# A decoder trunk's FFN down projection as a one-level Strassen product

## The chip, the cores and the metric

The kernel runs on one core of a Trainium2 chip. The metric is the device time of one execution in microseconds (us). Five engines work side by side, each with its own instruction stream: TensorE (PE, with its weight loads shown apart as PEld), VectorE (DVE), ScalarE (ACT), GpSimd (POOL) and SyncE (SP), which issues the DMAs.

## The reference

A trunk of two layers works on 512 tokens of width 1024 in float32. Layer 0 mixes tokens with a gated linear recurrence (HGRN2), layer 1 with sliding-window attention. Each mixer is followed by the same kind of feed-forward network, with D_FF = 2816, and a residual add:

```python
def conv_ffn(x, w_up, conv_w, conv_b, w_down):
    gate, val = jnp.split(x @ w_up, 2, axis=-1)
    gp = jnp.pad(gate, ((0, 0), (CONV_WIDTH - 1, 0), (0, 0)))
    conv = conv_b
    for j in range(CONV_WIDTH):
        conv = conv + conv_w[j] * gp[:, j:j + s_]
    return (jax.nn.silu(conv) * val) @ w_down
...
    h = h + conv_ffn(rms_norm(h, ffn_norm[layer]), ...)
```

The change is in the last product, `(...) @ w_down`: 512 tokens x 2816 features times 2816 x 1024 weights, in each layer. After layer 0 the residual stream goes into two norms (the shared K/V and the attention); after layer 1 into the final norm.

## The kernel before

All activations stand feature-major, as tiles of 128 features x 512 tokens. `h` holds the residual stream as eight such tiles. A product in near-float32 accuracy is made of three matmuls in the fp32r format: each operand x is split into a rounded part xh (an ACT copy) and the rest xl = x - xh (a DVE subtraction), and `three` (lines 103 to 106) adds hi*xh, hi*xl and lo*xh in PSUM. Weights come in raw by a DMA on SP's queue into one of four `raw` buffers of 128 x 1024, and `weights` (lines 91 to 101) makes `whi` (L99, ACT) and `wlo` (L100, DVE) from them, three buffers each. `project` loops over the k-tiles of one output tile.

The FFN has 22 tiles of 128 features. `hidden` makes one: 24 matmuls for the gate, 24 for the value, each with 512 columns, then the convolution on DVE (L497 to L502), SiLU on ACT (L503), a scaling on POOL (L504), the product with the value from PSUM on DVE (L505) and the split of the result (L507, L508). `up` makes a chunk of tiles, `down` multiplies the chunk with its rows of the weights: for each of the eight output tiles one PSUM bank, three matmuls a feature tile, and then `residual`: one DVE add of the bank to `h` (L192) and, where a norm follows, `norm.feed`: for each gain of the norm a scaled rounding on ACT (L138) and a split on DVE (L139), and a square on ACT (L147) that POOL adds up (L151). Layer 0 runs in two chunks of 11 tiles, and the second feeds the norm with two gains. Layer 1 runs in chunks of 10 and 8; its last four tiles go through `down_out`, which works on halves of 256 tokens and ends the kernel.

PSUM has eight banks: two under the tag `mm`, two under `bk`, which `any_bank` hands out in turn, and two pairs under `ax`. SBUF has 40 slots of 128 x 512 (`slot`) for the split activations. The order of instructions on an engine is set when the program is built, by a scheduler that may put an instruction ahead of earlier ones that are not ready; on the chip each engine works through its own list in that order.

Of the kernel before, what the change touches and what calls it, by code (L numbers as in the profile page):

```python
# [15 lines left out]
P = 128  # L16
# [28 lines left out]

@with_exitstack
def trunk(ctx: ExitStack, tc: tile.TileContext, xT, vec, w_qf, w_ig, w_ho, w_kv, w_q, w_o,
          w_up, w_dn, con, msk, out):
    nc = tc.nc
    V, A, G, PE = nc.vector, nc.scalar, nc.gpsimd, nc.tensor  # L50

# [15 lines left out]
    def slot(dt=F32):  # L67
        return act.tile([P, S], dt, tag="a", name=nm("a"))
# [12 lines left out]
    def any_bank():  # L81
        turn[0] += 1
        return mm_bank() if turn[0] % 2 else bk_bank()
# [107 lines left out]
    def residual(ps, m, norm):  # L191
        V.tensor_tensor(h[:, m], h[:, m], ps, op=ALU.add)  # L192
        if norm is not None:
            norm.feed(m)

    def project(ps, src, xs, n=KT, first=True, last=True, after={}):
        hi, lo = weights(src, n * P)
        for k in range(n):
            ks = slice(k * P, (k + 1) * P)
            three(ps, hi[:, ks], lo[:, ks], *xs[k], first and k == 0, last and k == n - 1)  # L200
            if k in after:
                after[k]()

# [1 line left out]
    norm = Norm([V_HG])  # L205

    lbe = small.tile([P, 2, HEADS], F32, tag="lbe", name="lbe", bufs=1)
# [276 lines left out]
        pair = aux_pair().rearrange("p (i a) b -> p i (a b)", i=2)  # L484
        return [pair[:, 0], pair[:, 1]]

# [1 line left out]
    def hidden(l, j, norm):  # L488
        xs = norm.xs[0]
        pg, pv = any_bank(), any_bank()  # L490
        project(pg, w_up[l, 2 * j], xs)
        if j == 0:
            norm.stats()
        project(pv, w_up[l, 2 * j + 1], xs, after={3: norm.spread} if j == 0 else {})
        gp = work("ks", (P, S + 2), 4)
        G.memset(gp[:, 0:2], 0.0)  # L496
        V.tensor_tensor(gp[:, 2:S + 2], pg, norm.bc, op=ALU.mult)  # L497
        cw = [col(V_CW + (l * 3 + i) * FT + j) for i in range(3)]
        c = work("qp", (P, S), 4)
        V.tensor_scalar(c, gp[:, 0:S], cw[0], col(V_CB + l * FT + j), op0=ALU.mult, op1=ALU.add)  # L500
        for i in (1, 2):
            V.scalar_tensor_tensor(c, gp[:, i:S + i], cw[i], c, op0=ALU.mult, op1=ALU.add)  # L502
        A.activation(c, c, AF.Silu)  # L503
        G.tensor_tensor(c, c, norm.bc, op=ALU.mult)  # L504
        V.tensor_tensor(c, pv, c, op=ALU.mult)  # L505
        uh, ul = slot(F32R), slot(F32R)
        A.copy(uh, c)  # L507
        V.tensor_tensor(ul, c, uh.bitcast(F32), op=ALU.subtract)  # L508
        return uh, ul

    def up(l, norm, j0, j1):
        return [hidden(l, j, norm) for j in range(j0, j1)]

    def down(l, hid, j0, nxt=None):
        n = len(hid)
        cut = n if n * P <= 1024 else (n + 1) // 2
        for m in range(KT):
            ps = any_bank()
            for a, b in ((0, cut), (cut, n)):
                if a < b:  # L520
                    project(ps, w_dn[l, m, :, (j0 + a) * P:(j0 + b) * P], hid[a:b], b - a,
                            a == 0, b == n)
            residual(ps, m, nxt)

    def down_out(l, hid, j0):
        n = len(hid) * P
        ws = []
        for m in range(KT):
            raw = wraw.tile([P, 1024], F32, tag="raw", name=nm("raw"))
            nc.sync.dma_start(raw[:, 0:n], w_dn[l, m, :, j0 * P:j0 * P + n])  # L530
            hi, lo = slot(F32R), slot(F32R)
            A.copy(hi[:, 0:n], raw[:, 0:n])
            V.tensor_tensor(lo[:, 0:n], raw[:, 0:n], hi[:, 0:n].bitcast(F32), op=ALU.subtract)
            ws.append((hi, lo))
# [70 lines left out]
    for m in (6, 7):  # L605
        Out(w_ho, m, m, [any_bank()]).run(mixed, nf)
    na = Norm([V_KV, V_AT])
    down(0, up(0, nf, 0, 11), 0)
    down(0, up(0, nf, 11, FT), 11, na)

# [1 line left out]
    halves = [slice(0, HD), slice(HD, P)]  # L612
    heads = lambda ap, g: ap.rearrange("p (t d) -> p t d", t=NT)[:, :, g * HD:(g + 1) * HD]
    k_hi, k_lo, v_hi, v_lo = ([slot(F32R) for _ in range(2)] for _ in range(4))
# [185 lines left out]
        o4.step(k, mixed[k])  # L800
    o4.close(nf)
    Out(w_o, 7, 7, [mm_bank()]).run(mixed, nf)
    down(1, up(1, nf, 0, 10), 0)
    hid = [up(1, nf, 10, 18), up(1, nf, 18, FT)]
    down(1, hid[0], 10)
    down_out(1, hid[1], 18)


def _pieces(w):
    """[K, N] -> per 128 columns: [N/128, 128 rows in the k-tile, K/128, 128]."""  # L810
    k, n = w.shape
    return np.ascontiguousarray(
        w.reshape(k // P, P, n // P, P).transpose(2, 1, 0, 3).reshape(n // P, P, k))


def _out_pieces(w):
    t = w.reshape(KT, P, D)
    a = t[:, :, :512].reshape(4, 2, P, 512).transpose(0, 2, 1, 3).reshape(4, P, D)
    b = t[:, :, 512:768].reshape(2, 4, P, 256).transpose(0, 2, 1, 3).reshape(2, P, D)
    return np.concatenate([a, b, _pieces(w)[6:]])  # L820


def _constants():
# [13 lines left out]
def _layout(x, hg_norm, hg_w_in, hg_lb_logits, hg_out_norm, hg_w_out, kv_norm, w_kv, attn_norm,  # L837
# [12 lines left out]
                           for j in range(8)])  # L850
    up = [np.stack([_pieces(w[:, :FF]), _pieces(w[:, FF:])], axis=1).reshape(2 * FT, P, D)
          for w in ffn_w_up]
    dn = [_pieces(w) for w in ffn_w_down]
    con, msk = _constants()
    arrays = dict(
        xT=x[0].T.reshape(KT, P, S).transpose(1, 0, 2), vec=vec, w_qf=qf, w_ig=ig,
        w_ho=_out_pieces(hg_w_out[0]), w_kv=_pieces(w_kv), w_q=_pieces(attn_w_q[0][:, perm]),
        w_o=_out_pieces(attn_w_o[0][perm]), w_up=np.stack(up), w_dn=np.stack(dn), con=con, msk=msk)
    return {k: np.ascontiguousarray(v) for k, v in arrays.items()}


# [14 lines left out]
```

## Time and profile before

| what | value |
|---|---|
| time, median of 3 runs (lowest to highest) | 1226.41 us (1226.07 to 1227.5) |
| profiled execution, span from first to last instruction | 1224.9 us |
| what lies around the span (median less span) | 1.5 us |
| PE busy | 1205.3 us (98%) |
| DVE, ACT, POOL busy | 58%, 37%, 14% |
| read from HBM | 102.33 MB, 85 GB/s over the span |

The span is the time from the first instruction's start to the last one's end in the one execution that was profiled. A share of busy time is an average over the whole span. Matmuls are pipelined and their ends are modelled, so the price of a matmul is read from the distance of one start to the next and not from its duration.

### The profile page before, as it was taken

The numbers are of one execution on the slowest core, as the hardware profiler recorded it, in microseconds if no ns is written. First come the engines' busy times: TensorE is split into PE (matmuls) and PEld (weight loads), VectorE is DVE, ScalarE is ACT, GpSimd is POOL, SyncE is SP. The second block draws the span as 40 slices with busy tenths as digits, with TensorE's granted clock in tenths as the row PEclk, the third lists the DMA queues.
The fourth block names the chain that finished last, engine by engine and source line by source line (L and its number), as shares of the span: only waits on it lengthen the run. The fifth ranks groups of instructions, "written<-read, shape, count | busy, mean of one in ns | idle before, by whom it ended". The sixth has DMA issues, their size and how long they took to land.

```text
span 1224.9 us, 15849 instructions
## 1 busy us (share of the span) xinstructions
PE 1205.3 (98%) x6154; PEld 1005.1 (82%) x6154; DVE 714.4 (58%) x1257; ACT 447.4 (37%) x814; POOL 176.2 (14%) x238
## 2 busy tenths in 40 slices
PE   8999999999999999999999999999999999999997
PEld 6888888888888888888888888887888888888886
DVE  7767676667555543555554778737555435565434
ACT  5433333325323222223233576734322222232223
POOL 3000000013201100001101243403101000111001
PEclk9999999999999999999999999999999999999998
DMA  7222222213233224333233311113322343323212
GB/s 241 73 69 70 70 70 70 69 35 104 87 95 94 77 82 116 103 92 99 76 84 115 104 36 53 35 52 104 103 86 71 87 119 103 103 86 103 83 55 69
DMA packets 34939, 105.45 MB, mean 86 GB/s; under 512 B 3760, under 2 KB 7088, under 8 KB 34864
## 3 DMA queue, kind: packets, MB, share of 16 engines
q1 hardware_dynamic: 33776, 103.40, 27.8%
q8 instruction: 48, 0.79, 0.3%
q10 hardware_dynamic: 1088, 1.05, 0.3%
q14 instruction: 27, 0.22, 0.1%
HBM read 102.33 MB, written 2.10 MB: 85 GB/s over the span
## 4 chain that ended last, share of the span: by engine, by line
PE 90%; DVE 4%; ACT 3%; issue 1%; POOL 1%; DMA 0%; SPq 0%; DVEq 0%; ACTq 0%; POOLq 0%
PE mm L104 13%; PE mm L106 13%; PE mm L105 13%; PE bk L104 11%; PE bk L106 11%; PE bk L105 11%; PE mm L251 7%; PE ax L319 3%; PE ax L106 2%; PE ax L104 2%; PE ax L105 2%; ACT ks L693 1%; DVE wlo L100 1%; ACT qp L693 1%; PE ax L378 1%
## 5 line engine op out<-in xcount | busy, mean ns | idle before, releaser
L99 ACT CAST whi<-raw 128x1024 fp32r<-128x1024 f32 (+3 forms) x208 | 199.1, 959 | 411.4 <-PE mm L105 184.1
L104 PE MATMUL mm<-a,whi 128*128 128x512 f32 x720 | 288.0, 400 | 0.0
L106 PE MATMUL mm<-a,wlo 128*128 128x512 f32 x720 | 285.8, 397 | 0.0
L105 PE MATMUL mm<-a,whi 128*128 128x512 f32 x720 | 285.2, 396 | 0.0
L100 DVE TENSOR_TENSOR wlo<-raw,whi 128x1024 fp32r<-128x1024 f32 (+3 forms) x208 | 237.6, 1143 | 68.8 <-ACT whi L99 68.7
L104 PE MATMUL bk<-a,whi 128*128 128x512 f32 x560 | 222.0, 396 | 0.0
L105 PE MATMUL bk<-a,whi 128*128 128x512 f32 x560 | 221.1, 395 | 0.3 <-DVE a L139 0.3
L106 PE MATMUL bk<-a,wlo 128*128 128x512 f32 x560 | 221.2, 395 | 0.0
L106 PEld LDWEIGHTS mm<-a,wlo 128*128 128x128 f32 x720 | 135.9, 189 | 31.1
L104 PEld LDWEIGHTS mm<-a,whi 128*128 128x128 f32 x720 | 136.0, 189 | 29.0 <-issue 0.2
L105 PEld LDWEIGHTS mm<-a,whi 128*128 128x128 f32 x720 | 136.0, 189 | 29.0 <-issue 0.2
L105 PEld LDWEIGHTS bk<-a,whi 128*128 128x128 f32 x560 | 105.5, 188 | 25.6 <-DVE a L139 0.7
L104 PEld LDWEIGHTS bk<-a,whi 128*128 128x128 f32 x560 | 105.5, 188 | 24.7 <-issue 0.5
L106 PEld LDWEIGHTS bk<-a,wlo 128*128 128x128 f32 x560 | 105.5, 188 | 24.5
L251 PE MATMUL mm<-whi,a 128*128 128x256 f32 x512 | 93.7, 283 | 0.0
L251 PEld LDWEIGHTS mm<-whi,a 128*128 128x128 f32 x512 | 79.5, 189 | 1.0 <-PE mm L123 0.4
L251 PE MATMUL mm<-wlo,a 128*128 128x256 f32 x256 | 72.5, 283 | 3.4 <-DVE wlo L100 3.4
L503 ACT ACTIVATE qp<-qp 128x512 f32<-128x512 f32 x44 | 27.8, 632 | 127.9 <-DVE qp L502 127.9
L504 POOL TENSOR_TENSOR qp<-qp,rbc 128x512 f32<-128x512 f32 x44 | 56.8, 1292 | 100.8 <-ACT qp L503 100.8
L496 POOL MEMSET ks<- 128x2 f32 x44 | 4.3, 100 | 448.7 <-DVE qp L502 435.2
L502 DVE SCALAR_TENSOR_TENSOR qp<-ks,vecs,qp 128x512 f32<-128x512 f32 x88 | 65.9, 749 | 1.7
L251 PEld LDWEIGHTS mm<-wlo,a 128*128 128x128 f32 x256 | 48.2, 188 | 4.6 <-DVE wlo L100 4.3
(198 smaller groups left out, 1395.6 us busy)
## 6 DMA issues: line engine op xcount, KB each, us to landing
raw<-in_w_up_dram SPq DMA_DIRECT2D x88, 512.0 KB, 3.5
raw<-in_w_dn_dram SPq DMA_DIRECT2D x32, 320.0 KB, 2.9
raw<-in_w_qf_dram SPq DMA_DIRECT2D x16, 512.0 KB, 3.6
raw<-in_w_ig_dram SPq DMA_DIRECT2D x14, 512.0 KB, 3.6
raw<-in_w_dn_dram SPq DMA_DIRECT2D x16, 384.0 KB, 3.2
raw<-in_w_ho_dram SPq DMA_DIRECT2D x8, 512.0 KB, 3.5
raw<-in_w_q_dram SPq DMA_DIRECT2D x8, 512.0 KB, 3.4
raw<-in_w_o_dram SPq DMA_DIRECT2D x8, 512.0 KB, 3.6
```

What stands on the lines that cost most here:

```text
L99: A.copy(hi[:, c], raw[:, c])
L100: V.tensor_tensor(lo[:, c], raw[:, c], hi[:, c].bitcast(F32), op=ALU.subtract)
L104: PE.matmul(ps, ah, bh, start=first, stop=False)
L105: PE.matmul(ps, ah, bl, start=False, stop=False)
L106: PE.matmul(ps, al, bh, start=False, stop=last)
L251: PE.matmul(ps, x[:, ts], w[:, ws], start=k == 0 and t % 2 == 0 and i == 0, stop=k == KT - 1 and t % 2 == 1 and i == 2, skip_group_check=True)
L319: PE.matmul(ps[:, c, 0:width], ks[:, c * P:(c + 1) * P], mv[:, c, 0:width], start=True, stop=True)
L378: PE.matmul(ps[r, c * b:(c + 1) * b], ks[:, o:o + b], qp[:, o + b:o + 2 * b], start=True, stop=True)
L502: V.scalar_tensor_tensor(c, gp[:, i:S + i], cw[i], c, op0=ALU.mult, op1=ALU.add)
L503: A.activation(c, c, AF.Silu)
L504: G.tensor_tensor(c, c, norm.bc, op=ALU.mult)
L693: A.activation(x, x, AF.Exp, bias=mx[:, n:n + 1], accum_out=den[:, n:n + 1])
```

## The change

The down projection of a pair of FFN tiles onto a pair of output tiles is a product of 2 x 2 blocks, with the 512 tokens cut into a left and a right half of 256. Instead of eight block products of 256 tokens the new kernel makes seven, each of three matmuls, from sums of weight blocks and of activation blocks (the form with S1 to S4 on the weights and four sums on the activations). `up_pairs` replaces `up` and makes the activation sums: half on DVE (`s3`), the others on POOL (`t13`, `t24`), and splits three tiles and a half in place of two. `blocks` loads four weight blocks (256 KB), makes four sums in three POOL adds, and splits 896 columns. `down` goes over four pairs of outputs; a pair uses four PSUM banks (mm and bk, or the two ax pairs, in turn), and its results are put together by eight DVE operations and one ACT copy. Chunks are of six tiles, and the last one of layer 0 of four; the last four tiles of layer 1 go through `down_out` as before, with their weights from an array of their own. `_quads` lays out the blocks on the host.

```diff
     def hidden(l, j, norm):
...
-        uh, ul = slot(F32R), slot(F32R)
-        A.copy(uh, c)
-        V.tensor_tensor(ul, c, uh.bitcast(F32), op=ALU.subtract)
-        return uh, ul
+        return c
+
+    def parts(x):
+        xh, xl = slot(F32R), slot(F32R)
+        A.copy(xh, x)
+        V.tensor_tensor(xl, x, xh.bitcast(F32), op=ALU.subtract)
+        return xh, xl
...
+    def up_pairs(l, norm, j0, j1):
+        out = []
+        for j in range(j0, j1, 2):
+            a = hidden(l, j, norm)
+            s3 = slot(F32R)
+            A.copy(s3[:, lft], a[:, lft])
+            V.tensor_tensor(s3[:, rgt], a[:, lft], s3[:, lft].bitcast(F32), op=ALU.subtract)
+            t13 = work("st")
+            G.tensor_tensor(t13[:, lft], a[:, lft], a[:, rgt], op=ALU.subtract)
+            b = hidden(l, j + 1, norm)
+            t24 = work("fr")
+            G.tensor_tensor(t13[:, rgt], a[:, rgt], b[:, rgt], op=ALU.subtract)
+            G.tensor_tensor(t24[:, lft], t13[:, rgt], a[:, lft], op=ALU.subtract)
+            G.tensor_tensor(t24[:, rgt], t24[:, lft], b[:, lft], op=ALU.add)
+            (b21, b22), (t1, t3), (t2, t4) = (both(parts(x)) for x in (b, t13, t24))
+            out.append(dict(p1=(s3[:, lft], s3[:, rgt]), p2=b21, p3=b22, p4=t4, p5=t1, p6=t2,
+                            p7=t3))
+        return out
+    A21, A12, A11, A22, S3, S1, S2, S4 = (slice(i * P, (i + 1) * P) for i in range(8))
+    LEFT = (("p1", A11), ("p2", A12), ("p4", A22), ("p3", S4), ("p5", S1), ("p6", S2), ("p7", S3))
+
+    def blocks(src):
...
+        nc.sync.dma_start(raw[:, 0:512], src)
+        two = lambda a, b: raw[:, a:b].rearrange("p (i c) -> p i c", i=2)
+        G.tensor_tensor(two(512, 768), two(256, 512),
+                        raw[:, A21].unsqueeze(1).broadcast_to([P, 2, P]), op=ALU.add)
+        G.tensor_tensor(raw[:, S2], raw[:, S1], raw[:, A11], op=ALU.add)
+        G.tensor_tensor(raw[:, S4], raw[:, S2], raw[:, A12], op=ALU.add)
+        A.copy(hi[:, P:], raw[:, P:])
+        V.tensor_tensor(lo[:, P:], raw[:, P:], hi[:, P:].bitcast(F32), op=ALU.subtract)
+        return hi, lo
 
     def down(l, hid, j0, nxt=None):
-        n = len(hid)
-        cut = n if n * P <= 1024 else (n + 1) // 2
-        for m in range(KT):
-            ps = any_bank()
-            for a, b in ((0, cut), (cut, n)):
-                if a < b:
-                    project(ps, w_dn[l, m, :, (j0 + a) * P:(j0 + b) * P], hid[a:b], b - a,
-                            a == 0, b == n)
-            residual(ps, m, nxt)
+        for q in range(KT // 2):
+            if q % 2 == 0:
+                banks = [mm_bank(), mm_bank(), bk_bank(), bk_bank()]
+            else:
+                banks = aux_two() + aux_two()
+            place = dict(p1=(0, lft), p3=(0, rgt), p2=(1, lft), p5=(1, rgt), p6=(2, lft),
+                         p7=(2, rgt), p4=(3, lft))
+            ps = {k: banks[b][:, s] for k, (b, s) in place.items()}
...
+            for i, x in enumerate(hid):
+                hi, lo = blocks(w_dn[l, j0 // 2 + i, q])
+                for k, w in LEFT:
...
+                    PE.matmul(ps[k], hi[:, w], xh, start=fresh, stop=False, skip_group_check=True)
+                    PE.matmul(ps[k], hi[:, w], xl, start=False, stop=False, skip_group_check=True)
+                    PE.matmul(ps[k], lo[:, w], xh, start=False, stop=last, skip_group_check=True)
+            h0, h1 = h[:, 2 * q], h[:, 2 * q + 1]
+            u = work("state")
+            V.tensor_tensor(h0, h0, banks[0], op=ALU.add)
+            V.tensor_tensor(h0, h0, banks[1], op=ALU.add)
+            V.tensor_tensor(h1[:, lft], h1[:, lft], ps["p4"], op=ALU.add)
+            V.tensor_tensor(h1[:, rgt], h1[:, rgt], ps["p5"], op=ALU.subtract)
+            A.copy(u[:, lft], ps["p6"])
+            V.tensor_tensor(u[:, lft], u[:, lft], ps["p1"], op=ALU.add)
+            V.tensor_tensor(u[:, rgt], u[:, lft], ps["p7"], op=ALU.subtract)
+            V.tensor_tensor(h0[:, rgt], h0[:, rgt], u[:, lft], op=ALU.add)
+            two = lambda x: x.rearrange("p (i t) -> p i t", i=2)
+            V.tensor_tensor(two(h1), two(h1), u[:, rgt].unsqueeze(1).broadcast_to([P, 2, H]),
+                            op=ALU.subtract)
+            for m in (2 * q, 2 * q + 1):
+                if nxt is not None:
+                    nxt.feed(m)
...
-    down(0, up(0, nf, 0, 11), 0)
-    down(0, up(0, nf, 11, FT), 11, na)
+    for j0, j1 in ((0, 6), (6, 12), (12, 18)):
+        down(0, up_pairs(0, nf, j0, j1), j0)
+    down(0, up_pairs(0, nf, 18, FT), 18, na)
...
-    down(1, up(1, nf, 0, 10), 0)
-    hid = [up(1, nf, 10, 18), up(1, nf, 18, FT)]
-    down(1, hid[0], 10)
+    for j0, j1 in ((0, 6), (6, 12)):
+        down(1, up_pairs(1, nf, j0, j1), j0)
+    hid = [up_pairs(1, nf, 12, 18), up(1, nf, 18, FT)]
+    down(1, hid[0], 12)
     down_out(1, hid[1], 18)
```

## Rows read from the trace of the kernel before

**Rows 1.** The page: busy us and share by engine; granted PE clock in 40 slices.

```profile
PE 1205.3 (98%) x6154; PEld 1005.1 (82%) x6154; DVE 714.4 (58%) x1257; ACT 447.4 (37%) x814; POOL 176.2 (14%) x238
...
PEclk9999999999999999999999999999999999999998
```

**Rows 2.** The page: the chain that ended last, by engine.

```profile
PE 90%; DVE 4%; ACT 3%; issue 1%; POOL 1%; DMA 0%; SPq 0%; DVEq 0%; ACTq 0%; POOLq 0%
```

**Rows 3.** Windows: layer 0's first down, its second down, and its first up projection.

```profile
core 0: us, PE busy (x) PEld busy (x) DVE busy (x) ACT busy (x) POOL busy (x), PEclk, DMA share, GB/s
436.40:497.00 60.60, 60.60 (x262) 49.13 (x262) 20.02 (x25) 13.10 (x17) 0.00 (x0) 1.00 0.38 105
620.30:681.00 60.70, 60.70 (x263) 49.23 (x262) 32.84 (x39) 26.09 (x38) 8.52 (x6) 1.00 0.36 104
...
326.00:436.00 110.00, 110.00 (x475) 89.16 (x475) 61.01 (x81) 33.25 (x41) 15.22 (x21) 1.00 0.29 87
```

**Rows 4.** Timeline of DVE in layer 0's first down (start, us, operation).

```profile
450.58 0.69 DVE L192 TENSOR_TENSOR h<-h,bk 128x512 f32<-128x512 f32 x1 [2.13 <-PE bk L106]
451.22 0.96 DVE L100 TENSOR_TENSOR wlo<-raw,whi 128x768 fp32r<-128x768 f32 x1
...
473.60 0.69 DVE L192 TENSOR_TENSOR h<-h,mm 128x512 f32<-128x512 f32 x1 [2.14 <-PE mm L106]
```

**Rows 5.** Timeline of PE in `down_out`, first and last of 36 starts.

```profile
1191.28 0.28 PE L104 MATMUL mm<-a,a 128*128 128x256 f32 x1
...
1195.60 0.28 PE L104 MATMUL bk<-a,a 128*128 128x256 f32 x1
```

**Rows 6.** Groups of instructions by line and shape, whole span: count, busy us, mean ns.

```profile
L504 POOL TENSOR_TENSOR qp<-qp,rbc 128x512 f32<-128x512 f32 x44 | 56.8, 1292 | 100.8 <-ACT qp L503 100.8
...
L508 DVE TENSOR_TENSOR a<-qp,a 128x512 fp32r<-128x512 f32 x44 | 30.2, 686 | 1.4 <-ACT a L507 1.4
...
L138 ACT ACTIVATE a<-h,vecs 128x512 fp32r<-128x512 f32 x40 | 28.4, 716 | 11.4 <-DVE h L192 9.3 <-DMA h<-in_xT_dram 1.6
...
L507 ACT CAST a<-qp 128x512 fp32r<-128x512 f32 x44 | 27.4, 622 | 15.2 <-DVE qp L505 14.9
...
L333 DVE TENSOR_TENSOR qp<-qp,tot 128x256 f32<-128x256 f32 x48 | 20.3, 423 | 4.6 <-PE ax L378 1.8 <-ACT mvb L356 0.5
...
L99 ACT CAST whi<-raw 128x768 fp32r<-128x768 f32 x16 | 13.4, 837 | 37.4 <-PE bk L105 20.8 <-PE mm L105 16.6
...
L545 DVE TENSOR_TENSOR h<-h,bk 128x256 f32<-128x256 f32 x8 | 3.4, 419 | 1.9 <-PE bk L106 1.8
```

**Rows 7.** Timeline of POOL, then of DVE, around four POOL adds.

```profile
835.32 6.72 POOL L151 TENSOR_TENSOR acc<-acc,kst 128x512 f32<-128x512 f32 x4 [6.61 <-ACT kst L147]
...
835.67 0.68 DVE L192 TENSOR_TENSOR h<-h,bk 128x512 f32<-128x512 f32 x1
...
840.88 2.25 DVE L100 TENSOR_TENSOR wlo<-raw,whi 128x1024 fp32r<-128x1024 f32 x1
...
843.64 1.21 DVE L100 TENSOR_TENSOR wlo<-raw,whi 128x1024 fp32r<-128x1024 f32 x1
```

**Rows 8.** Timelines at an FFN tile's end: PE's next matmul, then DVE's product.

```profile
507.55 0.40 PE L104 MATMUL mm<-a,whi 128*128 128x512 f32 x1
...
508.10 0.69 DVE L505 TENSOR_TENSOR qp<-bk,qp 128x512 f32<-128x512 f32 x1 [2.07 <-POOL qp L504]
```

**Rows 9.** Timelines at layer 0's end: DVE feeding the norm, then PE after the K projection.

```profile
651.53 0.75 DVE L139 SCALAR_TENSOR_TENSOR a<-h,vecs,a 128x512 fp32r<-128x512 f32 x1
...
680.64 0.69 DVE L192 TENSOR_TENSOR h<-h,bk 128x512 f32<-128x512 f32 x1
...
686.02 0.28 PE L175 MATMUL ax<-cons,acc 128*128 128x1 f32 x2
```

**Rows 10.** The page: DMA issues, KB each, us from issue to landing.

```profile
raw<-in_w_dn_dram SPq DMA_DIRECT2D x8, 256.0 KB, 2.7
```

## The prediction before the run

> **What bounds the kernel now.** I read the page first: PE is busy for 98% of the span at full granted clock [rows 1], and nine tenths of the chain that ended last is PE [rows 2]. The reader is to see that only PE time counts, as long as the other engines keep PE fed. Then I read the two kinds of stretch that the change touches. In a down projection PE never idles, DVE is a third to a half busy, and POOL does nothing unless a norm is being fed; in an up projection DVE is a little over half busy [rows 3]. Inside a down projection DVE works in short bursts: one residual add, then the low part of a weight tile, and from one residual add to the third after it, 3 x 33 = 99 matmuls, pass 23.02 us, so a 512-column matmul costs 0.2325 us [rows 4]. At the kernel's end the same three-matmul pattern runs with 256 columns: 36 matmuls in 4.32 us, 0.120 us each [rows 5].
>
> **What the change takes from PE.** Before, the projections through `down` hold 22 x 8 x 3 = 528 matmuls in layer 0 and 18 x 8 x 3 = 432 in layer 1: 960 x 0.2325 = 223.2 us. After, a pair of tiles and a pair of outputs is a block of 7 x 3 = 21 matmuls of 256 columns; 11 x 4 and 9 x 4 blocks make 80 x 21 = 1680 matmuls: 1680 x 0.120 = 201.6 us. PE saves 21.6 us. The weight is loaded once for each matmul [rows 1], in both kernels and in the rows, so the price already holds the load. The Trainium skill (TensorE: Matmul & The Clock Gate, Back-to-back issue gap) gives columns / 2.4 plus 2.5 ns: 215.8 and 109.2 ns, and so a saving of 23.7 us. Both rows are some 8 to 10% above that, and I keep the rows' 21.6.
>
> **What it adds to the other engines, per block.** PE needs 21 x 0.120 = 2.52 us. ACT rounds 896 columns, about 0.94 us by the 768-column row; DVE takes the low part of 896 columns, between 0.96 (768) and 1.22 (1024), so 1.09 us; POOL makes the four sums with one add of 256 and two of 128 [rows 6, 7]. No POOL add of these widths is in the trace: scaled from 1.29 us for 512 columns it is 0.65 + 2 x 0.32 = 1.29 us; if a quarter of the 512 price were fixed, 1.94 us. I take 1.5 us, nearer the scaled one. The load is 256 KB in 2.52 us, 104 GB/s, which the down stretches draw already [rows 3], and lands in 2.7 us [rows 10] with four raw buffers ahead: hidden.
>
> **Per quarter (one pair of outputs).** The residual chain is two 512-column adds from PSUM (0.69 each), four 256-column ones from PSUM (0.42), one of 256 (0.42) and one of 512 columns (0.69) with both inputs in SBUF [rows 4, 6]: 4.17 us, against two adds (1.4 us) before. A quarter of a six-tile chunk has three blocks: PE 7.56 us, DVE 3 x 1.09 + 4.17 = 7.44 us. DVE goes from idling half the time to 98%. What sits behind the chain on DVE is the low part of the next weights: `whi`/`wlo` have three buffers, so block i+3 starts on ACT when block i ends on PE, DVE may start about 1.3 us later, and PE needs the result 5.3 us after that end. If the chain runs first it ends some 3.6 us after the block's end and the low part at 4.7: in time by 0.6 us, with nothing else in the way.
>
> **POOL is in the way.** While POOL ran four adds from 835.32 to 842.04, a DVE add that read PSUM kept its 0.68 us, but a weight split with two SBUF inputs took 2.25 us, against 1.21 us for the next, just after POOL stopped; and the POOL adds took 1.68 us each against 1.29 alone [rows 6, 7]. So POOL's adds and DVE's two-SBUF-input operations take turns. In a six-tile chunk (PE 30.2 us) DVE has: the last gate product 0.69, three splits of the last pair 2.06, ten weight splits 10.9, three chains 12.5, two splits for the next up projection 2.4: 28.6 us, of which 9.9 read PSUM. POOL has three adds of the last pair, 2.0, and the sums of the six to eight blocks that four raw buffers don't let it do ahead, 9 to 12 us. Work that must take turns is 18.7 + 11 to 14 = 29.7 to 32.7 us. Below, the loss is 0 (all of it fits); above, if none of POOL's time fell beside a PSUM read, DVE would need 28.6 + 14 = 42.6 us and a chunk would lose 12. Since PSUM reads can cover 9.9 of POOL's 11 to 14, I take a value near full occupancy, 2 us a chunk, 12 us for the six; both ends go to the range, the upper one as 5 a chunk, since 12 would need POOL to work only beside two-input operations.
>
> **Each start of a chunk.** The first quarter takes all four mm/bk banks, and the fourth is the value bank of the last up tile, free when DVE's product ends: started 0.55 us after PE went on, 0.69 us long, so 1.3 us with the hand-over [rows 8]. PE reaches that bank after six matmuls, 0.72 us. Seven starts x 0.6 = 4.2 us (0.4 to 0.8 each). Behind the product stands the chain of the last pair: three POOL adds, a rounding and a split, ready some 5 us after PE went on. Two blocks of cover (5.0 us) hide it in a six-tile chunk; with its one block of cover the four-tile chunk doesn't, which is in its sum below.
>
> **The last chunk of layer 0.** It has two blocks a quarter, PE 8 x 2.52 = 20.2 us, and its residuals feed two gains of the next norm. Before, this feeding lay over 61 us of matmuls [rows 3], 7.67 us an output [rows 4]; it comes in full now. The K projection needs the first gain of all eight tiles, and the second gain of seven stands ahead of it on DVE. From the last up matmul DVE must do: product 0.69, three splits 2.06, six weight splits 6.5, four chains 16.7, one split of the K weights 1.22, fifteen feeds of 0.75 [rows 9] 11.2: 38.4 us. With 0.4 us ahead of it and the last three K matmuls behind (0.7 us) that ends at 39.5 us; PE alone would end at 20.2 + 5.6 = 25.8 us, and before there was no idle time in these 5.6 us (the last residual at 680.64, the K projection done by 686.02) [rows 9]. So at least 13.7 us are lost. POOL's seven square sums (9 us), pair adds and block sums come on top, partly beside 12.9 us of PSUM reads: 0 to 10 us, of which I take 3, near the lower end by the same cover as above. 17 us. ACT has 16 roundings of 0.72 [rows 6] and its other work, some 26 us, below DVE.
>
> **The rest.** `down_out` is unchanged but for its source. Its eight splits of weights (0.69 each) used to lie in DVE's idle time; now the chunk ahead has none, and its first half takes PE 96 x 0.120 = 11.5 us against DVE's last chain 4.2, splits 5.5 and own adds 5.5: 0 to 3.7 us, I take 2. In the up projections a pair adds 1.1 us on DVE, 1.0 on ACT and 2.6 on POOL to 22.3 us of matmuls, beside a DVE that is 55% busy there [rows 3]: nothing; without that cover it would be 1.1 us x 20 pairs. Slots: 16 + 21 + 8 exceed 40 at layer 1's end, so the last tiles' splits wait until the norm's slots come free during tile 21; their consumer is a whole chunk away: nothing.
>
> **Sum.** -21.6 + 12 + 4.2 + 17 + 2 = +13.6 us. The profiled execution spans 1224.9 us; the runs' median is 1226.41, so 1.5 us lie around the span, and I keep them: 1240 us. What a measurement can tell from no change is about 0.2%, 2.5 us.
>
> **Rivals.**
> (a) *DVE and POOL fit, PE alone sets the chunks.* The six-tile chunks and `down_out` lose nothing (the upper figures, 28.6 of 30.2 us, allow it), and the last chunk loses its 13.7, or 8.5 if the second gain's feeds are put off: -21.6 + 4.2 + 13.7 = -3.7, or -8.9 us: 1217 to 1223. For it: 0.6 us of slack in each quarter and sums made early. Against it: the turns of POOL and DVE [rows 7]. It decides if all the six-tile chunks together lose less than about 1 us (6 with the feeds put off). 0.22.
> (b) *Turns in every quarter.* Two-SBUF-input work and POOL strictly one after the other: 3.27 + 1.11 + 3 x 1.5 = 8.9 us against 7.56, in 24 quarters +32 us: -21.6 + 4.2 + 32 + 17 + 2 = +33.6, 1260 us. For it, the 2.25 us split; against it, that the sums of the first four to six blocks and the last chain lie outside the chunk. 0.18. Beside it stands the Trainium skill (SBUF — State Buffer, Who interferes with whom): a VectorE instruction with two SBUF inputs and a GpSimd one that reads SBUF exclude each other for the whole instruction. The trace agrees: 1.04 us were lost in 1.16 us beside POOL.
> (c) *It cancels:* stalls of 19 to 24 us, 1226 us. 0.12.
> That 256-column matmuls cost more than half of the wide ones, so that nothing is saved, [rows 5] exclude.
> My forecast, a few us lost in each chunk and DVE the bound in the last one of layer 0, has 0.48 (its own range 1229 to 1252).
>
> **Numbers.** Faster 0.22 (a), same 0.12 (c), slower 0.48 + 0.18 = 0.66. The range reaches from (a) to (b): 1219 to 1260; some 0.1 lies below and as much above. PE gaps in the last chunk may lower the granted clock, 1.00 in all stretches of [rows 3]; that is part of the upper end.
>
> **What would show it.** Right: 256-column starts 0.120 us apart inside blocks; PE waiting for `wlo` after the second and third quarters of six-tile chunks; weight splits over 2 us beside POOL adds; DVE without idle time from layer 0's last up tile until some 40 us later, and the K projection ending 13 us or more late. Wrong: `wlo` never late, narrow POOL adds well under 1.3 us a block, or an instruction order that puts splits ahead of chains and feeds.

## The result and the profile after

The changed kernel takes 1236.33 us in the median of four executions (1232.21 to 1239.02) against 1226.24 for the kernel before: ratio 1.008, 95% interval 1.0059 to 1.010. It is slower, by 10 us or 0.8%; 1240 us was forecast. The execution that the profile shows is the quickest of the four, 1232.21 us with a span of 1230.4, so its trace explains 5.5 of the 10 us.

The page of the changed kernel, with busy shares, the granted clock in 40 slices and the chain that ended last:

```profile
PE 1192.5 (97%) x6874; PEld 1027.1 (83%) x6874; DVE 891.2 (72%) x1513; ACT 502.3 (41%) x906; POOL 470.8 (38%) x558
...
PEclk9999999999999999999999899999999999999998
...
PE 70%; DVE 12%; POOL 8%; ACT 5%; issue 3%; DMA 2%; SPq 0%; DVEq 0%; POOLq 0%; ACTq 0%
```

Against [rows 1, 2], DVE has risen from 58 to 72% of the span and POOL from 14 to 38%. PE's share of the chain has fallen by 20 points, and 15 of them went to DVE and POOL. The windows of the first down chunk and of the stretch from the last up matmul of layer 0 to the norm's statistics say where:

```profile
core 0: us, PE busy (x) PEld busy (x) DVE busy (x) ACT busy (x) POOL busy (x), PEclk, DMA share, GB/s
379.00:410.80 31.80, 30.80 (x254) 30.14 (x253) 28.82 (x40) 13.90 (x18) 22.37 (x25) 1.00 0.38 115
653.60:701.40 47.80, 36.99 (x215) 32.41 (x213) 43.07 (x60) 25.99 (x40) 19.93 (x20) 0.89 0.27 88
```

Where [rows 3] had PE without a gap and DVE a third to a half busy, a six-tile chunk now has DVE at 28.8 of 31.8 us; in the last chunk of layer 0 DVE works 43.1 of 47.8 us and PE only 37.0, partly at the lower clock. From first start to the chunk's end the six six-tile chunks take 31.8, 32.2, 31.8, 31.7, 31.7 and 31.0 us, against 30.24 of matmuls: 8.8 us lost. The last chunk and the K projection need 20.2 + 5.6 = 25.7 us of matmuls, and their stretch takes 22.1 us more than that. A part comes back in the attention, from one statistics start to the next. The lines are the two starts, then the window of this stretch in the kernel before, in the changed kernel and in the run e2 (below):

```profile
701.35 0.27 PE L175 MATMUL ax<-cons,acc 128*128 128x1 f32 x1 [0.82 <-POOL acc L151]
...
858.31 0.38 PE L175 MATMUL ax<-cons,acc 128*128 128x1 f32 x2 [0.40 <-POOL acc L151]
...
686.02:846.71 160.69, 156.97 (x879) 131.62 (x878) 113.64 (x287) 96.55 (x243) 52.20 (x89) 0.99 0.19 58
701.35:858.31 156.96, 152.14 (x858) 126.42 (x858) 113.58 (x289) 96.51 (x243) 55.04 (x92) 1.00 0.18 58
...
683.87:843.18 159.31, 155.58 (x880) 130.62 (x878) 113.61 (x287) 96.49 (x243) 52.27 (x89) 1.00 0.20 57
```

That is 157.0 us, against 160.7 before (686.02 to 846.71). Two things lie in these 3.7 us. The changed kernel has run 21 matmuls of the V projection, 4.9 us of PE time, ahead of the statistics: its window of the last chunk counts 215 matmuls, where 168 of the product and 24 of the K projection make 192, and its attention counts 21 fewer than before. And the kernel before had a granted clock of 0.99 in its attention against 1.00; e2, with the work of the kernel before there and a clock of 1.00, takes 159.3 us, so about 1.4 of the 3.7 us are not owed to the change, and some 2.3 of the V projection's 4.9 come back. The account -21.6 + 8.8 + 22.1 - 3.7 = +5.6 us meets the spans, 1230.4 - 1224.9 = +5.5.

What PE waits for at the start of a six-tile chunk shows in the timelines of PE, POOL and DVE at the second chunk of layer 1:

```profile
1019.89 0.39 PE L106 MATMUL mm<-a,wlo 128*128 128x512 f32 x1
1020.12 0.28 PE L579 MATMUL mm<-a,whi 128*128 128x256 f32 x1
...
1020.95 0.28 PE L580 MATMUL mm<-a,whi 128*128 128x256 f32 x1
1022.18 0.39 PE L579 MATMUL mm<-a,whi 128*128 128x256 f32 x1 [0.95 <-DVE qp L505]
...
1019.41 0.74 POOL L553 TENSOR_TENSOR raw<-raw 128x256 f32<-128x256 f32 x1
1020.11 1.29 POOL L504 TENSOR_TENSOR qp<-qp,rbc 128x512 f32<-128x512 f32 x1
...
1021.43 0.69 DVE L505 TENSOR_TENSOR qp<-mm,qp 128x512 f32<-128x512 f32 x1 [2.17 <-POOL qp L504]
```

Inside a block the starts are 0.12 us apart, as [rows 5] had it. Then PE stands for 1.1 us until the last tile's product (L505) frees a bank. That product began 0.55 us after PE went on in [rows 8]; here 1.31 us after, because POOL's scaling L504 came behind a block sum (L553). The first two chunks of layer 1 then wait 0.5 us for an operand. In layer 0 a chunk's start shows three shorter waits: 0.3 us for the bank and two for the operands made from `t24`, 1.6 us together. These two are, in the first chunk, the waits for the operand's high part and for its low part:

```profile
385.87 0.39 PE L579 MATMUL bk<-a,whi 128*128 128x256 f32 x1 [0.52 <-ACT a L510]
386.59 0.39 PE L580 MATMUL bk<-a,whi 128*128 128x256 f32 x1 [0.34 <-DVE a L511]
```

The chunk began at 379.08, so the low part was there only some 7.5 us after PE went on. Within the quarters PE waits hardly at all, as its waits over the whole span show (who waits for whom: us in total, times, the longest):

```profile
PE mm L104 <- DVE h L587: 4.5, 1, 4.5
...
PE bk L579 <- ACT a L510: 3.4, 4, 1.9
PE mm L579 <- DVE qp L505: 2.8, 3, 1.0
PE bk L580 <- DVE a L511: 1.6, 5, 0.3
...
PE mm L581 <- DVE wlo L558: 1.4, 1, 1.4
...
PE ax L581 <- DVE wlo L558: 0.3, 1, 0.3
```

The second to fourth of these lines are waits at the starts, those of the last chunk among them. For a Strassen block's `wlo` (L558) PE waits twice in the kernel, 1.4 us in the last chunk and 0.3 us in a six-tile one.

Groups by line and shape, first of the changed kernel (weight split, then POOL's three block sums), then POOL's sums of one block in its timeline, with little beside them:

```profile
L558 DVE TENSOR_TENSOR wlo<-raw,whi 128x896 fp32r<-128x896 f32 x80 | 100.8, 1275 | 3.3 <-ACT whi L557 2.2
...
L555 POOL TENSOR_TENSOR raw<-raw 128x128 f32<-128x128 f32 x80 | 73.1, 913 | 5.8
L553 POOL TENSOR_TENSOR raw<-raw 128x256 f32<-128x256 f32 x80 | 66.9, 836 | 49.2 <-DMA raw<-in_w_dn_dram 41.4 <-issue 4.2 <-DVE h L587 2.9
L556 POOL TENSOR_TENSOR raw<-raw 128x128 f32<-128x128 f32 x80 | 62.4, 780 | 6.3
...
667.33 0.74 POOL L553 TENSOR_TENSOR raw<-raw 128x256 f32<-128x256 f32 x1 [5.37 <-DMA raw<-in_w_dn_dram]
668.14 0.46 POOL L555 TENSOR_TENSOR raw<-raw 128x128 f32<-128x128 f32 x1
668.68 0.47 POOL L556 TENSOR_TENSOR raw<-raw 128x128 f32<-128x128 f32 x1
```

A block's sums cost 1.67 us with little in the way and 2.53 us on average; the split that was taken at 1.09 us costs 1.27 on average. Both engines pay for working side by side; with POOL's sums left out the split falls back to 1.09 us (e4 below).

The last chunk, in DVE's and POOL's timelines and the one long wait of PE:

```profile
674.95 1.08 DVE L558 TENSOR_TENSOR wlo<-raw,whi 128x896 fp32r<-128x896 f32 x1
675.95 1.78 DVE L139 SCALAR_TENSOR_TENSOR a<-h,vecs,a 128x512 fp32r<-128x512 f32 x1
...
687.47 2.31 DVE L100 TENSOR_TENSOR wlo<-raw,whi 128x1024 fp32r<-128x1024 f32 x1
...
698.82 3.02 DVE L139 SCALAR_TENSOR_TENSOR a<-h,vecs,a 128x512 fp32r<-128x512 f32 x2 [0.39 <-ACT a L138]
...
675.84 3.01 POOL L151 TENSOR_TENSOR acc<-acc,kst 128x512 f32<-128x512 f32 x2 [4.96 <-ACT kst L147]
...
698.32 2.97 POOL L151 TENSOR_TENSOR acc<-acc,kst 128x512 f32<-128x512 f32 x2 [9.63 <-ACT kst L147]
...
682.40 0.77 PE L104 MATMUL mm<-a,whi 128*128 128x512 f32 x1 [4.51 <-DVE h L587]
```

DVE goes from one operation to the next almost without idle time, the splits of the norm that run beside POOL's square sums (L151) take 1.2 to 1.8 us in place of 0.75 [rows 9], and PE waits 4.5 us at one place for a residual add that stands in DVE's list. That wait is for a bank of the K projection, whose first two matmuls stand in PE's list ahead of 38 matmuls of the last quarter; DVE is busy all through it. After this wait, and after one of 2.0 us at the chunk's start, PE goes on at the lower of its two clock levels (1.2 GHz): narrow matmuls start 0.21 us apart in place of 0.12, until 688.3 us here.

### The profile page after: what moved, and what is told of

It reads as the page before. It is cut to its first block, busy times and chain, and to the rows that moved or that the text cites. A ratio compares the mean times of both kernels' runs of the same rounds, so it can differ in the third digit from the quotient of the medians.

```text
span 1230.4 us, 18185 instructions
## 1 busy us (share of the span) xinstructions
PE 1192.5 (97%) x6874; PEld 1027.1 (83%) x6874; DVE 891.2 (72%) x1513; ACT 502.3 (41%) x906; POOL 470.8 (38%) x558
## 4 chain that ended last, share of the span: by engine, by line
PE 70%; DVE 12%; POOL 8%; ACT 5%; issue 3%; DMA 2%; SPq 0%; DVEq 0%; POOLq 0%; ACTq 0%
PE mm L104 8%; PE mm L105 8%; PE mm L106 8%; PE mm L251 7%; PE bk L105 6%; PE bk L104 6%; PE bk L106 6%; PE ax L319 3%; PE ax L581 3%; PE ax L579 2%; PE ax L580 2%; DVE wlo L100 2%; POOL qp L504 2%; PE ax L106 2%; PE ax L104 2%
## 5 line engine op out<-in xcount | busy, mean ns | idle before, releaser
L104 PE MATMUL mm<-a,whi 128*128 128x512 f32 x560 | 225.1, 402 | 5.2 <-DVE h L587 4.5
L99 ACT CAST whi<-raw 128x1024 fp32r<-128x1024 f32 (+1 forms) x152 | 153.8, 1015 | 185.8 <-PE mm L105 72.0
L106 PE MATMUL mm<-a,wlo 128*128 128x512 f32 x560 | 222.3, 397 | 0.0
L105 PE MATMUL mm<-a,whi 128*128 128x512 f32 x560 | 222.0, 397 | 0.0
L100 DVE TENSOR_TENSOR wlo<-raw,whi 128x1024 fp32r<-128x1024 f32 (+1 forms) x152 | 188.7, 1245 | 12.9 <-ACT whi L99 12.6
L104 PE MATMUL bk<-a,whi 128*128 128x512 f32 x400 | 158.5, 396 | 0.0
L105 PE MATMUL bk<-a,whi 128*128 128x512 f32 x400 | 158.1, 395 | 0.2 <-DVE a L139 0.2
L105 PEld LDWEIGHTS mm<-a,whi 128*128 128x128 f32 x560 | 105.7, 189 | 22.1 <-issue 0.5
L557 ACT CAST whi<-raw 128x896 fp32r<-128x896 f32 x80 | 74.8, 941 | 91.1 <-POOL raw L556 42.5
L558 DVE TENSOR_TENSOR wlo<-raw,whi 128x896 fp32r<-128x896 f32 x80 | 100.8, 1275 | 3.3 <-ACT whi L557 2.2
L105 PEld LDWEIGHTS bk<-a,whi 128*128 128x128 f32 x400 | 75.3, 188 | 18.4 <-DVE a L139 0.7
L553 POOL TENSOR_TENSOR raw<-raw 128x256 f32<-128x256 f32 x80 | 66.9, 836 | 49.2 <-DMA raw<-in_w_dn_dram 41.4
L579 PE MATMUL ax<-a,whi 128*128 128x256 f32 x280 | 80.2, 286 | 1.2 <-DVE state L589 0.7
L581 PE MATMUL ax<-a,wlo 128*128 128x256 f32 x280 | 80.2, 287 | 0.3 <-DVE wlo L558 0.3
```

Source lines behind the costliest of these rows:

```text
L99: A.copy(hi[:, c], raw[:, c])
L100: V.tensor_tensor(lo[:, c], raw[:, c], hi[:, c].bitcast(F32), op=ALU.subtract)
L104: PE.matmul(ps, ah, bh, start=first, stop=False)
L105: PE.matmul(ps, ah, bl, start=False, stop=False)
L106: PE.matmul(ps, al, bh, start=False, stop=last)
L553: G.tensor_tensor(two(512, 768), two(256, 512), raw[:, A21].unsqueeze(1).broadcast_to([P, 2, P]), op=ALU.add)
```

## The experiments

Times are medians; each run had the kernel before beside it (1225.4 to 1226.5 us), and the ratio is to that. That spread of 1 us is also about what can be told between two runs of the table.

| run | what | us | ratio, 95% interval |
|---|---|---|---|
| (the change) | | 1236.3 | 1.0080 [1.0059, 1.0100] |
| e1_plain4 | last four tiles of layer 0 without Strassen | 1224.8 | 0.9989 [0.9979, 0.9999] |
| e2_plain10 | last ten tiles of layer 0 without Strassen | 1219.3 | 0.9940 [0.9923, 0.9957] |
| e3_order | other order of the seven products | 1232.5 | 1.0051 [1.0032, 1.0070] |
| e4_nosums | no POOL sums of weight blocks | 1230.1 | 1.0021 [1.0004, 1.0037] |
| e5_late_gain | second gain fed after the last chunk | 1229.7 | 1.0039 [1.0025, 1.0054] |
| e8_one_gain | second gain left out | 1227.6 | 1.0017 [1.0007, 1.0026] |
| e9_chunks_only | kernel before with the new chunks | 1233.1 | 1.0069 [1.0054, 1.0084] |
| e7_plain10_order | e2 and e3 | 1220.0 | 0.9958 [0.9943, 0.9972] |
| e10_plain10_dve | e2, three activation sums on DVE | 1218.2 | 0.9936 [0.9923, 0.9948] |
| e11_plain10_dve_order | e10 and e3 | 1215.8 | 0.9917 [0.9903, 0.9930] |
| e12_plain10_gate | e11, and L504 on DVE | 1212.0 | 0.9879 [0.9862, 0.9895] |

**The last chunk: e1 and e2.**

```diff
-    for j0, j1 in ((0, 6), (6, 12), (12, 18)):
+    for j0, j1 in ((0, 6), (6, 12)):                  # e1 keeps (12, 18)
         down(0, up_pairs(0, nf, j0, j1), j0)
-    down(0, up_pairs(0, nf, 18, FT), 18, na)
+    down_plain(up(0, nf, 12, FT), na)                 # e1: up(0, nf, 18, FT)
...
+    def down_plain(hid, nxt=None):                    # the old down, weights of its own
...
+                    project(ps, w_d0[m, :, a * P:b * P], hid[a:b], b - a, a == 0, b == n)
+            residual(ps, m, nxt)
```

> The changed kernel, but the last four tiles of layer 0 go through the old down projection (512 columns, one output at a time, norm fed as before). Theory A (the loss sits in the last Strassen chunk of layer 0, where DVE has 43 us of work in the 47.8 us from the last up matmul to the end of the K projection; the six-tile chunks pay only at their start): those 47.8 us become 28 to 32 (PE 22.3 + 5.6 us, DVE about 25), so 12 to 16 us off the changed kernel's 1236 (median): 1220 to 1224, just under the kernel before. Theory B (POOL's adds and DVE's splits take turns in every quarter and the six-tile chunks pay for it too): only one chunk in seven is undone, 3 to 5 us off: 1231 to 1233.

> The same with the last ten tiles of layer 0 in one chunk through the old down projection, so that the feeding of the norm has 58 us of matmuls beside it; Strassen chunks are left for tiles 0 to 11 of layer 0 and 0 to 17 of layer 1. Theory A: the ten tiles give back 3.2 us of PE time (72 wide matmuls of 0.2325 us as 126 narrow ones of 0.120... in the third chunk less 18, i.e. 33.5 - 30.2 us) and one chunk start of 1.6 us goes, but the last chunk now hides all of DVE's feeding: 1218 to 1223, within 3 us of the run with four plain tiles. Theory B: two chunks of seven undone, 8 to 12 us off: 1224 to 1228.

Both came out on theory A's side, 11.5 and 17.0 us off: e1 ends 0.8 us above A's range, e2 inside it, though 5.5 us below e1 where at most 3 were expected. (The 33.5 and 30.2 us in that expectation are 144 wide and 252 narrow matmuls, not 72 and 126.) With ten plain tiles there is no gap of PE around the K projection, and the kernel is faster than the kernel before and the changed one: 60 blocks save 16.2 us (720 x 0.2325 - 60 x 2.52), and the five six-tile chunks lose 8.3 in the trace (31.7 to 32.1 us each): 7.9 us, of which 7.2 were measured.

**The chunk lengths alone: e9.**

```diff
-    down(0, up(0, nf, 0, 11), 0)
-    down(0, up(0, nf, 11, FT), 11, na)
+    for j0, j1 in ((0, 6), (6, 12), (12, 18)):        # in the kernel before; layer 1 alike
+        down(0, up(0, nf, j0, j1), j0)
+    down(0, up(0, nf, 18, FT), 18, na)
```

> The kernel before with the new chunks and nothing of Strassen: six tiles a chunk and the last one of layer 0 of four, all with 512-column matmuls. Theory A (short chunk and Strassen chain together make the last chunk's loss): feeding two gains over 22 us of matmuls instead of 61 costs some 5 us, as it does with four plain tiles in the Strassen kernel (K projection 33.0 us after the last up matmul against 27.9 of PE), the other chunks cost nothing: 1229 to 1233. Theory B (the chunk of four is the whole loss, whatever its product is): 1240 or more.

Measured 1233.1, at the edge of A's range: the new chunks cost 7.6 us without any Strassen product. The window from the last up matmul of layer 0 to the statistics, and the waits of PE in the K projection:

```profile
657.40:690.80 33.40, 29.77 (x123) 23.11 (x123) 30.26 (x35) 21.86 (x35) 12.88 (x12) 0.97 0.40 126
...
686.32 0.50 PE L105 MATMUL mm<-a,whi 128*128 128x512 f32 x1 [1.33 <-DVE a L139]
...
689.79 0.80 PE L105 MATMUL mm<-a,whi 128*128 128x512 f32 x1 [2.30 <-DVE a L139]
```

The stretch holds 27.9 us of matmuls, so the chunk of four loses 5.5 us there; the rest of the 7.6 was not traced to a place. DVE is busy for 30.3 of 33.4 us: feeding two gains for eight tiles fills it as soon as only 22 us of matmuls stand beside it, and PE waits for DVE's splits of the last tiles. What the Strassen chain and its sums add in that chunk is, by the medians, the difference of the change and e1, 11.5 us, and the 2.2 us of matmuls that they save: 13.7 us, with what the clock costs in either.

**What fills DVE in the last chunk: e5 and e8.**

```diff
-                    nxt.feed(m)                       # e5
+                    nxt.feed(m, part=0)
+        if nxt is not None:
+            for m in range(KT):
+                nxt.feed(m, False, part=1)
...
-            for i, g in enumerate(self.gains):        # e8
+            for i, g in enumerate(self.gains[:1]):
...
-            three(pq, hi[:, ks], lo[:, ks], *na.xs[1][k], k == 0, k == KT - 1)
+            three(pq, hi[:, ks], lo[:, ks], *na.xs[0][k], k == 0, k == KT - 1)
```

> The changed kernel, but during the last Strassen chunk of layer 0 only the first gain of the next norm is fed; the eight roundings and splits of the second gain come after the chunk's last quarter. Theory A (DVE is the bound of that chunk): seven splits of 0.75 us no longer stand ahead of the K projection, which ends 4 to 6 us earlier; what comes later has PE work beside it: 1230 to 1233 against 1236 (median). Theory B (the chain of each quarter and the order of instructions set the end, not DVE's sum): within 2 us of the changed kernel.

> The changed kernel with the second gain of that norm left out altogether: the queries are projected from the tiles with the first gain, so 8 roundings and 8 splits are gone. Theory A: the K projection ends about 5 to 7 us earlier and the time falls as much: 1229 to 1231; what is left of the last chunk's loss, some 12 us, is the residual chain of eight DVE operations a quarter with only 5 us of PE time beside it. Theory B: under 3 us off.

6.6 and 8.7 us off by the medians, 5.9 and 8.0 against the kernel before of each: theory A, with e8 a little above its figures. The windows of the same stretch, of e5 and then of e8:

```profile
654.10:695.10 41.00, 34.10 (x213) 29.55 (x212) 37.05 (x54) 22.74 (x35) 20.42 (x20) 0.96 0.32 103
...
653.70:696.60 42.90, 36.47 (x216) 31.66 (x214) 36.18 (x53) 21.89 (x33) 20.55 (x22) 0.92 0.31 98
```

Seven or eight splits of 0.75 us fewer on DVE take 6.0 to 6.9 us from its busy time and 4.9 to 6.8 from the stretch, so the stretch gets shorter with DVE's work. It is not DVE's sum alone: e8 has 0.9 us less of it than e5 and takes 1.9 us longer, at a lower clock. PE's clock is 0.96 in e5 and 0.92 in e8, against 0.89 in the changed kernel. In both runs the K projection's first matmul stands ahead of only 17 matmuls of the chunk and waits 1.8 us, for a weight, in place of 4.5; what that order gave by itself was not tried.

**POOL's block sums: e4.**

```diff
-        G.tensor_tensor(two(512, 768), two(256, 512),
-                        raw[:, A21].unsqueeze(1).broadcast_to([P, 2, P]), op=ALU.add)
-        G.tensor_tensor(raw[:, S2], raw[:, S1], raw[:, A11], op=ALU.add)
-        G.tensor_tensor(raw[:, S4], raw[:, S2], raw[:, A12], op=ALU.add)
-        A.copy(hi[:, P:], raw[:, P:])
-        V.tensor_tensor(lo[:, P:], raw[:, P:], hi[:, P:].bitcast(F32), op=ALU.subtract)
+        wide = lambda x: x.rearrange("p (i c) -> p i c", i=2)
+        src2 = raw[:, 0:448].unsqueeze(1).broadcast_to([P, 2, 448])
+        A.copy(wide(hi[:, P:]), src2)
+        V.tensor_tensor(wide(lo[:, P:]), src2, wide(hi[:, P:]).bitcast(F32), op=ALU.subtract)
```

> The changed kernel without POOL's three adds a block: the sums of weight blocks are left out, and ACT and DVE split the same 896 columns, read from the loaded columns instead (two times 448), so PE, ACT, DVE and DMA have the same number of instructions and sizes. Theory A: PE does not wait inside the six-tile chunks, so POOL's adds cost nothing there; only the chunk starts and the last chunk get a little shorter: 0 to 5 us off. Theory B (taking turns with POOL costs the chunks): the splits fall from 1.27 to 1.09 us and 10 us or more go: under 1226.

6.2 us off in the median, between the two: A's "0 to 5" was too little, B's 10 too much. The ten executions spread from 1225.0 to 1232.5 us, and the one in the trace is among the slowest, with a span of 1230.7. The split's group, and the first chunk's first matmul, last matmul and the next up matmul:

```profile
L555 DVE TENSOR_TENSOR wlo<-raw,whi 128x896 fp32r<-128x896 f32 x80 | 86.4, 1085 | 10.8 <-ACT whi L554 9.4
...
379.43 0.28 PE L576 MATMUL mm<-a,whi 128*128 128x256 f32 x1
...
410.22 0.39 PE L104 MATMUL mm<-a,whi 128*128 128x512 f32 x1
```

The split falls to the 1.09 us of the forecast, the six chunks to 30.8 or 30.9 us each, 5.4 us less in all. So POOL's block sums do cost the six-tile chunks, 0.2 to 1.3 us each, and mainly at the starts: the bank wait falls from 1.1 to 0.4 us in the first two chunks of layer 1 and goes in layer 0. Whether POOL's own list or the turns with DVE delay the start, this run doesn't tell, since both go with the sums.

**The start of a chunk: e3, e7, e10, e11, e12.**

```diff
-    LEFT = (("p1", A11), ("p2", A12), ("p4", A22), ("p3", S4), ("p5", S1), ("p6", S2), ("p7", S3))
+    LEFT = (("p1", A11), ("p2", A12), ("p3", S4), ("p5", S1), ("p7", S3), ("p6", S2), ("p4", A22))
-                    last = i == len(hid) - 1 and k in ("p3", "p4", "p5", "p7")
+                    last = i == len(hid) - 1 and k in ("p3", "p4", "p5", "p6")     # e3, e7, e11, e12
...
-            G.tensor_tensor(t13[:, rgt], a[:, rgt], b[:, rgt], op=ALU.subtract)
-            G.tensor_tensor(t24[:, lft], t13[:, rgt], a[:, lft], op=ALU.subtract)
-            G.tensor_tensor(t24[:, rgt], t24[:, lft], b[:, lft], op=ALU.add)
+            V.tensor_tensor(t13[:, rgt], a[:, rgt], b[:, rgt], op=ALU.subtract)      # e10 to e12
+            V.tensor_tensor(t24[:, lft], t13[:, rgt], a[:, lft], op=ALU.subtract)
+            V.tensor_tensor(t24[:, rgt], t24[:, lft], b[:, lft], op=ALU.add)
...
-        G.tensor_tensor(c, c, norm.bc, op=ALU.mult)
+        V.tensor_tensor(c, c, norm.bc, op=ALU.mult)   # L504: e12
```

> The changed kernel with the seven products of a block in another order (p1, p2, p3, p5, p7, p6, p4), so that the fourth bank and the operands that POOL finishes last (t2, t4) are wanted at the end of a block. Theory A: the trace shows 1.5 to 2.0 us of PE waits at the start of each chunk, for p4's bank and for t4; of these some 1.0 to 1.4 us go in each of six chunks: 6 to 9 us off the changed kernel, 1227 to 1230. Theory B (the waits at the starts only move POOL's and DVE's work, which bounds the chunk): within 2 us of the changed kernel.

> The run with ten plain tiles at layer 0's end, plus the other order of the seven products. The order alone gave no shorter chunks in the trace (31.3 to 32.1 us against 31.0 to 32.2), so the waits at a chunk's start look like part of what POOL and DVE need for the chunk and not a cost of their own: within 1.5 us of the 1219.3 without the order. If the starts are a cost of their own, 5 us less: 1214.

> The run with ten plain tiles at layer 0's end, with the three activation sums that wait for the second tile of a pair (one half of t13, both of t24) on DVE in place of POOL. At a chunk's start POOL's three sums took 1.58, 1.07 and 1.06 us, while DVE needs about 0.42 each: the operand that PE waits for at the start comes some 2.4 us earlier and two of the waits there (0.69 and 0.61 us) go. If they are the cost, 1.0 to 1.3 us in each of four or five chunks: 1214 to 1216 against 1219.3. If POOL's and DVE's turns only shift the loss into the quarters, as with the other order of products: within 1.5 us of 1219.

> The same with the other order of the seven products (p1, p2, p3, p5, p7, p6, p4) as well, which also takes the wait for the fourth bank (0.3 to 0.4 us). With the operand early, the order adds 0.3 us a chunk at most: 1213 to 1216; if the quarters take it back, no less than the run without it.

> The run before it (ten plain tiles, three activation sums on DVE, the other order of products) with the gate's scaling L504 on DVE as well, in every FFN tile. In the changed kernel this POOL operation ends 1.3 us after PE has gone on to the down projection, behind a block sum on POOL, and the bank that PE waits for at a chunk's start comes free only after it. If POOL's queue at the start is the cost, 0.7 to 1.4 us go in each of five starts: 1209 to 1213 against 1215.8. If DVE, with 44 operations of 0.69 us more in the up projections, is then late itself, no gain or a loss: 1215 to 1220.

The order alone is a miss for theory A: 3.9 us off the median instead of 6 to 9, hardly shorter six-tile chunks (31.1 to 32.1 us, 0.7 us less in all), and nothing at all on top of e2, as e7's first reading had it. B's 2 us were missed too, but the profiled executions span the same, 1230.3 and 1230.4 us. The order shortened the starts of layer 0, and PE waited for a Strassen block's `wlo` eight times in place of two, most of them inside six-tile chunks; six of the eight in e3's waits:

```profile
PE ax L581 <- DVE wlo L558: 1.7, 6, 0.6
```

So most of that loss moved from the starts into the quarters. The three sums (three of the four, all on POOL in the changed kernel: `s3` is only the split of half a tile) on DVE alone gave 1 us, where 3 to 5 were hoped for, so e10's second reading holds; both together 3.4 us; with the scaling on DVE 7.3 us. e11 and e12 came out in the ranges of their first readings. The first chunk of e12, and DVE and PE at its second chunk of layer 1:

```profile
379.02 0.28 PE L579 MATMUL mm<-a,whi 128*128 128x256 f32 x1
...
409.18 0.39 PE L104 MATMUL mm<-a,whi 128*128 128x512 f32 x1
...
1001.56 0.69 DVE L504 TENSOR_TENSOR qp<-qp,rbc 128x512 f32<-128x512 f32 x1 [0.70 <-ACT qp L503]
1002.36 0.69 DVE L505 TENSOR_TENSOR qp<-mm,qp 128x512 f32<-128x512 f32 x1
...
1001.94 0.28 PE L579 MATMUL mm<-a,whi 128*128 128x256 f32 x1
...
1002.77 0.28 PE L580 MATMUL bk<-a,whi 128*128 128x256 f32 x1
1003.10 0.39 PE L579 MATMUL mm<-a,whi 128*128 128x256 f32 x1
```

The chunk takes 30.2 us, the time of its 252 matmuls; at the second chunk of layer 1 the product begins 0.42 us after PE went on in place of 1.31, and the wait at the bank falls from 1.1 to 0.2 us. With that four of the five Strassen chunks take 30.1 to 30.6 us, the time of PE alone within 0.3 us. The last one of layer 1 takes 30.9: it still waits 0.9 us for a bank. The kernel is the best one run, 1.2% under the kernel before.

## Why the prediction was right

The kernel became slower, by 10 us where 14 were forecast, and the time lies in the range. Of the two losses that decided it, one was where the prediction put it and the other was not, and that the total came so near is in part luck.

- **PE saves 21.6 us.** Right: narrow matmuls start 0.12 us apart, and a chunk freed of waits takes 30.2 us. (The two starts of [rows 5] are the first and the last of 37, with 36 distances between them, so 0.120 stands.)
- **The last chunk, 17 us.** The mechanism was right: DVE is the bound. Its work was summed at 38.4 us and POOL's turns at 3, and 43.1 us were measured. Two things are in the 43.1 that the sum had otherwise: the fifteen feeds took 15.9 us in place of 11.2, and DVE split three tiles of the following weights there and not one. The stretch was 22.1 us longer than its matmuls, of which 3.7 came back in the attention, 18.4 net; some 1.4 of the 3.7 are the clock of the kernel before. The sign that was named for it came: the K projection's last matmul starts at 700.1 us, 20.8 us after all its matmuls could have been done. Weight splits over 2 us came only once there, at the 2.31 us of the next projection's weights; a Strassen block's split takes 1.64 us at most. That a short chunk by itself loses 5.5 us (e9) is contained in the sum, which put the feeding of the norm beside 20 us of matmuls.
- **The starts, 4.2 us, and the six-tile chunks, 12 us.** Together 15.6 us for the six chunks, 8.8 measured in the trace. The split was wrong: PE waits 1.1 to 1.8 us at each start, not 0.6, and hardly at all in the quarters. Two steps failed at the start. One took the first bank's release from [rows 8], as if POOL's scaling would still come on time; it comes behind a block sum on POOL, and the bank costs 0.4 us a chunk in layer 0 and 1.1 to 1.2 in layer 1. The other said that two blocks of cover hide the chain of the last pair: it was put at 5 us and took some 7.5, since POOL's three sums alone took 3.7 us in place of 2.0, and cost 1.4 us a chunk in layer 0. The step that put PE's waits for `wlo` into the second and third quarters failed too: the six-tile chunks have one such wait, of 0.3 us. When e3 took waits out of the starts, such waits did come; that the starts give DVE and POOL the lead that keeps the quarters free fits this, but is not shown. That POOL's block sums are a cause of the waits at the starts is shown by e4, and that the scaling on POOL is one by e12. e12 also has more work on DVE and yet chunks at PE's time, so DVE's sum in a six-tile chunk was not the bound.
- **`down_out`, 2 us.** Nothing: from its first matmul to the last one of the kernel pass 28.7 us in both kernels.
- **Rivals.** (b), turns in every quarter, is ruled out by the 31.8 us chunks; (a) failed at the last chunk and at the starts.

The terms thus measure -21.6 + 8.8 + 18.4 = +5.6 us, against +13.6 forecast: less than half. The median lies another 4 us above the profiled execution, and no term of the sum stands for them; the prediction named a lower clock only for the upper end of its range. The other three executions have mean granted clocks of 0.986 to 0.990 against 0.993 and are 3 to 7 us longer. None of the three has a trace, but the traced executions of e3 and e4, which keep the last Strassen chunk, have such clocks (0.989 and 0.987). The last chunk of e3, then the attention of e4:

```profile
652.85:698.47 45.62, 38.18 (x207) 33.27 (x206) 42.97 (x59) 26.18 (x40) 20.37 (x19) 0.81 0.30 91
...
697.69:857.90 160.21, 156.03 (x858) 129.98 (x858) 113.58 (x289) 96.61 (x243) 53.58 (x92) 0.97 0.19 57
```

Against the changed kernel's trace (0.89 and 1.00) e3 loses clock in the last chunk and e4 in the attention, where it takes 3.2 us longer with as many matmuls. So both places can lose it; which of them did in the three executions stays open.

## What to carry to other kernels

Fewer matmuls pay only where the other engines' work per matmul has room: count each engine's work for the shortest stage, not for the mean one, since here a chunk of four tiles that also feeds a norm cost some 18 us while the chunks of six took 3 to 6% more than PE's time. Leave the stage with the most side work on the plain product, as e2 did. Work that is put on an idle engine (POOL) is not free if a short operation on the critical hand-over queues behind it or is slowed beside it: moving that one operation (L504) and three sums off POOL, with another order of the products, was worth 7.3 us.

## What the runs showed of the hardware

POOL's two-input adds cost 0.46 and 0.74 us for 128 and 256 columns with little beside them, and a 512-column product 1.29 [rows 6]. An estimate from these three: about 0.19 us are fixed and each column costs 2.2 ns, so halving the width does not halve the price. Over the whole kernel, with DVE's two-input operations beside them, the 128-column ones average 0.78 and 0.91 us and the 256-column one 0.84. PE's granted clock was 1.00 from the last up matmul of layer 0 to the statistics in e2, where PE never waits:

```profile
622.50:683.87 61.37, 61.37 (x265) 49.37 (x263) 37.26 (x43) 28.47 (x42) 11.54 (x11) 1.00 0.40 114
```

It was 0.89 in the changed kernel, where PE stood for up to 4.5 us at a time: there the stretch lost PE time to the waits and again to the clock after them.
